# Row-wise softmax over a large vocabulary: stores on ScalarE's queue, loads on SyncE's, hand-placed semaphores and scaling on VectorE

## The chip, the cores and the metric

The kernel runs on one core of one Trainium2 chip. The metric is device time in microseconds of one execution. The core has TensorE (not used here), VectorE (DVE), ScalarE (ACT), GpSimd (POOL), SyncE (SP) and 16 DMA engines that move data between the chip's memory (HBM) and the on-chip memory (SBUF, 128 partitions). Instructions that start a DMA sit in the in-order instruction stream of one engine; here SP's, and after the change SP's and ACT's.

## What is computed

The input is 16 x 256 rows of 32768 float32 logits; the output has the same shape.

```python
scaled = logits / temperature                      # temperature is 1.0
scaled = scaled - scaled.max(axis=-1, keepdims=True)
exp_scaled = np.exp(scaled)
out = exp_scaled / exp_scaled.sum(axis=-1, keepdims=True)
```

Input and output are 536.87 MB each, so 1073.74 MB have to pass the DMA engines once.

## The kernel before

Each row is cut into two halves of 16384 columns, and each half lies on a partition of its own, so 128 partitions hold 64 rows. That is a group; there are G = 64 groups. A group is processed as C = 2 chunks of 8192 columns: one chunk is a tile of 128 x 8192 float32, 32 KiB on each partition, 4 MiB in all. A pool holds six such tiles (`_BUFS`). A chunk is loaded, worked on in place, and stored from the same tile.

For each chunk, `exps` runs a DVE reduce (line 107) that gives the negated maximum of the 8192 columns, and an ACT exponential (line 114) over the chunk, with that maximum as bias and the sum of the exponentials as a second output. When both chunks of a group are through, `factors` finds the factor of each chunk: a DVE minimum over the two negated maxima (line 129); `combine`, a shuffle and a two-operand step that exchanges this value between the two partitions of a row (lines 84 and 87); a small ACT exponential `ee` of the chunk maximum against the row maximum (line 131); a DVE multiply-and-sum of `ee` and the chunk sums (line 138); a second `combine`, of the row sums; a reciprocal (line 149) and the product `f` of `ee` and the reciprocal (line 150). Then `scales` multiplies the chunk by its factor: the first 4096 columns on DVE (line 160, one scalar per partition), the other 4096 on ACT (a Copy with a scale, line 163).

All DMAs are issued by SP, in program order (`keep_in_program_order`): loads at line 64, stores at line 75. The list `order` sets this order: six loads first, then store 0, and from there on store i followed by load i+5. A load waits until its tile is free, that is until the store from that tile has landed; a store waits until both scalings are done. Because SP works in order, load i+5 stands behind store i, and store i+1 behind load i+5. In the first group the loads, and in the last group loads, stores, reduces, exponentials and scalings, are cut into pieces of 4096 columns (`_LAST_DMA`).

Semaphores and the order of instructions on DVE and ACT are set by the framework's scheduler; `factors` has high priority. In the middle of the run, DVE does: the reduce of a group's second chunk, the first exchange, (wait for ACT) multiply-and-sum, second exchange, reciprocal, `f`, the two scalings, and then the reduce of the next group's first chunk.

Of the kernel before, what the change touches and what calls it, by code (L numbers as in the profile page):

```python
# [6 lines left out]


_SPLIT = 2
_CW = 8192  # L10
_BUFS = 6
_PIECE = 8192
_LAST_DMA = 4096
_DVE_SHARE = 0.5


@with_exitstack
def kernel(
    ctx: ExitStack,
    tc: tile.TileContext,  # L20
    logits: bass.AP,
    temperature: bass.AP,
    out: bass.AP,
):
    nc = tc.nc
    inv_t = 1.0 / float(temperature)
    P = nc.NUM_PARTITIONS
    fp32 = mybir.dt.float32
    Exp = mybir.ActivationFunctionType.Exp
    Copy = mybir.ActivationFunctionType.Copy  # L30
    X = mybir.AxisListType.X
    A = mybir.AluOpType

    xf = logits.flatten_outer_dims()
    of = out.flatten_outer_dims()
    N, V = xf.shape
    W = V // _SPLIT
    CW = min(_CW, W)
    C = W // CW
    assert W * _SPLIT == V and CW * C == W and (N * _SPLIT) % P == 0  # L40
    x = xf.rearrange("n (h v) -> (n h) v", h=_SPLIT)
    o = of.rearrange("n (h v) -> (n h) v", h=_SPLIT)
    G = N * _SPLIT // P
    n_chunks = G * C
    n_rounds = _SPLIT.bit_length() - 1

    xpool = ctx.enter_context(tc.tile_pool(name="x", bufs=_BUFS))
    spool = ctx.enter_context(tc.tile_pool(name="stats", bufs=3))
    slots = {}
    stats = {}  # L50

    def spans(total: int, step: int) -> list[tuple[int, int]]:
        return [(s, min(step, total - s)) for s in range(0, total, step)]

    def piece(g: int) -> int:
        return _PIECE if g < G - 1 else min(_PIECE, _LAST_DMA)

    def load(i: int) -> None:
        g, c = divmod(i, C)
        xs = xpool.tile([P, CW], fp32, tag="x", name="xs")  # L60
        slots[i] = xs
        for s, n in spans(CW, _LAST_DMA if g in (0, G - 1) else CW):
            tc.keep_in_program_order(
                nc.sync.dma_start(  # L64
                    out=xs[:, s : s + n],
                    in_=x[g * P : (g + 1) * P, c * CW + s : c * CW + s + n],
                )
            )

    def store(i: int) -> None:  # L70
        g, c = divmod(i, C)
        xs = slots.pop(i)
        for s, n in spans(CW, _LAST_DMA if g == G - 1 else CW):
            tc.keep_in_program_order(
                nc.sync.dma_start(  # L75
                    out=o[g * P : (g + 1) * P, c * CW + s : c * CW + s + n],
                    in_=xs[:, s : s + n],
                )
            )

    def combine(v, op) -> None:
        for j in range(n_rounds):
            mask = [i ^ (1 << j) for i in range(32)]
            nc.vector.stream_shuffle(  # L84
                out=v[:, j + 1 : j + 2], in_=v[:, j : j + 1], mask=mask
            )
            nc.vector.tensor_tensor(  # L87
                out=v[:, j + 1 : j + 2],
                in0=v[:, j : j + 1],
                in1=v[:, j + 1 : j + 2],  # L90
                op=op,
            )

    def exps(i: int) -> None:
        g, c = divmod(i, C)
        xs = slots[i]
        ps = spans(CW, piece(g))
        K = C * len(ps)
        if c == 0:
            stats[g] = tuple(  # L100
                spool.tile([P, K], fp32, tag=f"{nm}{K}", name=nm)
                for nm in ("nm", "ssum", "ee", "f", "ttj")
            )
        nm, ssum = stats[g][:2]
        for j, (s, n) in enumerate(ps):
            k = c * len(ps) + j
            nc.vector.tensor_reduce(  # L107
                out=nm[:, k : k + 1], in_=xs[:, s : s + n], axis=X, op=A.max, negate=True
            )
            if inv_t != 1.0:  # L110
                nc.vector.tensor_scalar_mul(
                    out=nm[:, k : k + 1], in0=nm[:, k : k + 1], scalar1=inv_t
                )
            nc.scalar.activation(  # L114
                out=xs[:, s : s + n],
                in_=xs[:, s : s + n],
                func=Exp,
                bias=nm[:, k : k + 1],
                scale=inv_t,
                accum_out=ssum[:, k : k + 1],  # L120
            )

    def factors(g: int) -> None:
        nm, ssum, ee, f, ttj = stats[g]
        nMh = spool.tile([P, 1 + n_rounds], fp32, tag="nMh", name="nMh")
        Sh = spool.tile([P, 1 + n_rounds], fp32, tag="Sh", name="Sh")
        rS = spool.tile([P, 1], fp32, tag="rS", name="rS")
        with tc.high_priority():
            nc.vector.tensor_reduce(out=nMh[:, 0:1], in_=nm, axis=X, op=A.min)  # L129
            combine(nMh, A.min)  # L130
            nc.scalar.activation(  # L131
                out=ee,
                in_=nm,
                func=Exp,
                bias=nMh[:, n_rounds : n_rounds + 1],
                scale=-1.0,
            )
            nc.vector.tensor_tensor_reduce(  # L138
                out=ttj,
                in0=ee,  # L140
                in1=ssum,
                scale=1.0,
                scalar=0.0,
                op0=A.mult,
                op1=A.add,
                accum_out=Sh[:, 0:1],
            )
            combine(Sh, A.add)
            nc.vector.reciprocal(out=rS, in_=Sh[:, n_rounds : n_rounds + 1])  # L149
            nc.vector.tensor_scalar_mul(out=f, in0=ee, scalar1=rS)  # L150

    def scales(i: int) -> None:
        g, c = divmod(i, C)
        xs = slots[i]
        f = stats[g][3]
        ps = spans(CW, piece(g))
        for j, (s, n) in enumerate(ps):
            k = c * len(ps) + j
            cut = int(n * _DVE_SHARE) // 512 * 512
            nc.vector.tensor_scalar_mul(  # L160
                out=xs[:, s : s + cut], in0=xs[:, s : s + cut], scalar1=f[:, k : k + 1]
            )
            nc.scalar.activation(  # L163
                out=xs[:, s + cut : s + n],
                in_=xs[:, s + cut : s + n],
                func=Copy,
                scale=f[:, k : k + 1],
            )

    order = [("L", i) for i in range(min(_BUFS, n_chunks))] + [("S", 0)]  # L170
    for i in range(1, n_chunks):
        order.append(("S", i))
        if i + _BUFS - 1 < n_chunks:
            order.append(("L", i + _BUFS - 1))

    nxt = 0
    done = -1
    loaded = 0
    for kind, i in order:
        if kind == "L":  # L180
            load(i)
            loaded = i + 1
        else:
            g = i // C
            if g > done:
                while nxt < (g + 1) * C:
                    assert nxt < loaded
                    exps(nxt)
                    nxt += 1
                factors(g)  # L190
                done = g
            scales(i)
            store(i)


# [33 lines left out]
```

## Time and profile before

| | |
|---|---|
| Time, median of 3 runs | 2495.66 us (2494.19 to 2496.56) |
| Profiled execution: span, first to last instruction | 2493.8 us (the profile gives no other time of it) |
| Instructions | 2234 |
| DVE busy | 1487.4 us, 60% of the span |
| ACT busy | 1405.0 us, 56% of the span |
| DMA, mean over the span | 431 GB/s |
| DVE reduce, 128x8192 (line 107) | 8682 ns each |
| ACT exponential, 128x8192 (line 114) | 7121 ns each |
| DVE scaling, 128x4096 (line 160) | 2350 ns each |
| ACT scaling, 128x4096 (line 163) | 3701 ns each |
| Store of 4 MiB, issue to landing | 38.2 us (median) |
| Load of 4 MiB, issue to landing | 29.0 us (median) |

How to read it: the span is the time between the first and the last instruction of one profiled execution. "Busy" is the time in which an engine ran a compute instruction; issuing a DMA or waiting is not counted. "DMA share" in a stretch is the mean share in which the 16 DMA engines had a packet under way. In this kernel a data packet is one partition's run of a tile, 32 KiB for a whole chunk. q1 is the queue on which SP issues; q14 carries instructions. The chain of work is followed back from the last instruction to what released it, step by step. Times in stretches and timelines count from the start of the span.

### The profile page before, as it was taken

What the parts mean: (1) busy time and instruction counts of PE and PEld (TensorE: products, weight loads), DVE (VectorE), ACT (ScalarE), POOL (GpSimd) and SP (SyncE); (2) the same over time, 40 slices, a digit from 0 to 9 for tenths busy, and PEclk for the clock granted to TensorE, in tenths of its full rate; (3) what the DMA queues carried; (4) which work ended last, traced back from release to release, by engine and by line L of the source; (5) the groups of instructions that cost most, each with busy time, mean ns of one, the idle gap of its engine ahead of it and who ended that gap; (6) DMA issues with size and microseconds to landing.
All of it is one profiled execution on the core that took longest, in us unless ns stands there. A gap on an engine that the chain in (4) does not pass through costs nothing.

```text
span 2493.8 us, 2234 instructions
## 1 busy us (share of the span) xinstructions
DVE 1487.4 (60%) x964; ACT 1405.0 (56%) x455; POOL 0.2 (0%) x4
## 2 busy tenths in 40 slices
DVE  7655565556655566555665566655666566655663
ACT  5665554655556555565555655555546555465553
POOL 0000000000000000000000000000000000000000
DMA  9999999999999999999999999999999999999998
GB/s 412 433 430 432 429 431 432 433 433 434 433 434 432 435 432 435 432 435 431 436 431 435 432 434 433 434 433 433 433 433 433 433 433 434 434 433 434 432 431 368
DMA packets 37745, 1073.90 MB, mean 431 GB/s; under 512 B 4192, under 2 KB 4192, under 8 KB 4192
## 3 DMA queue, kind: packets, MB, share of 16 engines
q1 hardware_dynamic: 37728, 1073.76, 99.9%
q14 instruction: 17, 0.14, 0.0%
HBM read 536.87 MB, written 536.87 MB: 431 GB/s over the span
## 4 chain that ended last, share of the span: by engine, by line
DMA 96%; SPq 1%; ACT 1%; DVE 1%; issue 1%; ACTq 0%
DMA out_dram<-xs 93%; DMA xs<-in_logits_dram 2%; SPq L64 1%; DVE nm L107 1%; ACT xs L163 1%; ACT xs L114 0%; ACTq L224 0%; SPq L75 0%; DVE f L150 0%; ACT ee L131 0%; DVE rS L149 0%; DVE Sh L87 0%; DVE ttj L138 0%; DVE Sh L84 0%; DVE Sh L138 0%
## 5 line engine op out<-in xcount | busy, mean ns | idle before, releaser
L114 ACT ACTIVATE xs<-xs,nm 128x8192 f32<-128x8192 f32 (+1 forms) x130 | 912.1, 7016 | 972.4 <-DVE nm L107 972.4
L107 DVE TENSOR_REDUCE nm<-xs 128x1 f32<-128x8192 f32 (+1 forms) x130 | 1111.6, 8551 | 527.3 <-DMA xs<-in_logits_dram 527.3
L163 ACT ACTIVATE xs<-xs,f 128x4096 f32<-128x4096 f32 (+1 forms) x130 | 468.1, 3648 | 71.4 <-DVE f L150 71.4
L160 DVE TENSOR_SCALAR xs<-xs,f 128x4096 f32<-128x4096 f32 (+1 forms) x130 | 295.7, 2318 | 3.7 <-DVE f L150 1.8
L138 DVE CUSTOM_DVE_ANT_0 ttj<-ee,ssum 128x2 f32<-128x2 f32 x64 | 10.3, 161 | 423.8 <-ACT ee L131 423.8
L114 ACT ACTIVATION_READ_ACCUMULATOR xs<-xs,nm 128x1 f32 x130 | 24.2, 186 | 0.0
L131 ACT ACTIVATE ee<-nm,nMh 128x2 f32<-128x2 f32 x64 | 17.9, 280 | 0.0
L150 DVE TENSOR_SCALAR f<-ee,rS 128x2 f32<-128x2 f32 x64 | 14.6, 229 | 2.2
L149 DVE RECIPROCAL rS<-Sh 128x1 f32<-128x1 f32 x64 | 10.5, 164 | 2.2
L87 DVE TENSOR_TENSOR nMh<-nMh 128x1 f32<-128x1 f32 x64 | 10.2, 160 | 2.2
L87 DVE TENSOR_TENSOR Sh<-Sh 128x1 f32<-128x1 f32 x64 | 10.2, 160 | 2.2
L129 DVE TENSOR_REDUCE nMh<-nm 128x1 f32<-128x2 f32 x64 | 9.9, 155 | 2.2
L84 DVE STREAM_SHUFFLE nMh<-nMh 128x1 f32<-128x1 f32 x64 | 9.7, 151 | 0.0
L84 DVE STREAM_SHUFFLE Sh<-Sh 128x1 f32<-128x1 f32 x64 | 9.7, 151 | 0.0
L114 ACT ACT_TABLE_LOAD x1 | 1.3, 1283 | 12.9 <-DMA xs<-in_logits_dram 12.9
L138 DVE DVE_READ_ACCUMULATOR2_ANT Sh<- 128x1 f32 x64 | 5.3, 84 | 0.0
L84 DVE LOAD_MASK_SELECT Sh<-Sh x64 | 0.9, 14 | 2.8
L84 DVE LOAD_MASK_SELECT nMh<-nMh x64 | 0.9, 14 | 2.7
L210 POOL MEMSET const-bfloat16-1.0<- 128x1 bf16 x1 | 0.1, 102 | 0.0
L210 POOL MEMSET const-uint8-127<- 128x1 uint8 x1 | 0.1, 102 | 0.0
L210 POOL MEMSET const-float32-0.0<- 128x1 f32 x1 | 0.1, 99 | 0.2 <-issue 0.2
L210 POOL MEMSET const-float32-1.0<- 128x1 f32 x1 | 0.1, 99 | 0.0
## 6 DMA issues: line engine op xcount, KB each, us to landing
out_dram<-xs SPq DMA_DIRECT2D x126, 4096.0 KB, 38.2
xs<-in_logits_dram SPq DMA_DIRECT2D x124, 4096.0 KB, 29.0
xs<-in_logits_dram SPq DMA_DIRECT2D x8, 2048.0 KB, 22.3
out_dram<-xs SPq DMA_DIRECT2D x4, 2048.0 KB, 26.7
```

Of the source, the lines that this page charges most:

```text
L64: nc.sync.dma_start(out=xs[:, s : s + n], in_=x[g * P : (g + 1) * P, c * CW + s : c * CW + s + n],)
L84: nc.vector.stream_shuffle(out=v[:, j + 1 : j + 2], in_=v[:, j : j + 1], mask=mask)
L87: nc.vector.tensor_tensor(out=v[:, j + 1 : j + 2], in0=v[:, j : j + 1], in1=v[:, j + 1 : j + 2], op=op,)
L107: nc.vector.tensor_reduce(out=nm[:, k : k + 1], in_=xs[:, s : s + n], axis=X, op=A.max, negate=True)
L114: nc.scalar.activation(out=xs[:, s : s + n], in_=xs[:, s : s + n], func=Exp, bias=nm[:, k : k + 1], scale=inv_t, accum_out=ssum[:, k : k + 1],
L129: nc.vector.tensor_reduce(out=nMh[:, 0:1], in_=nm, axis=X, op=A.min)
L131: nc.scalar.activation(out=ee, in_=nm, func=Exp, bias=nMh[:, n_rounds : n_rounds + 1], scale=-1.0,)
L138: nc.vector.tensor_tensor_reduce(out=ttj, in0=ee, in1=ssum, scale=1.0, scalar=0.0, op0=A.mult, op1=A.add, accum_out=Sh[:, 0:1],)
L149: nc.vector.reciprocal(out=rS, in_=Sh[:, n_rounds : n_rounds + 1])
L150: nc.vector.tensor_scalar_mul(out=f, in0=ee, scalar1=rS)
L160: nc.vector.tensor_scalar_mul(out=xs[:, s : s + cut], in0=xs[:, s : s + cut], scalar1=f[:, k : k + 1])
L163: nc.scalar.activation(out=xs[:, s + cut : s + n], in_=xs[:, s + cut : s + n], func=Copy, scale=f[:, k : k + 1],)
```

## The change

- The tile framework's scheduling is switched off for the body (`tile_critical`); the six chunk buffers, the statistics and all semaphores are allocated by hand. `Stream` stands for an engine's own semaphore, counted up by one by each of its compute instructions, and leaves out a wait that an earlier wait already covers. `Landing` stands for a DMA semaphore: two per buffer for loads (one per piece of 4096 columns), one per buffer for stores.
- Stores are issued by ACT instead of SP. ACT's order in a group is: two exponentials, `ee`, (wait for the first scaling) store, (wait for the second) store.
- Loads alone stay on SP. Load i+6 waits for the landing of store i, from the same buffer, and for nothing else.
- One exchange per group: negated maxima and sums of a group lie side by side in one tile `t`, and one shuffle gives each partition its partner's maxima and sums. The minimum, `ee` and the multiply-and-sum then run over both halves' values (4 columns, 8 in the last group), and the second exchange and the product `f` are gone.
- Scaling is done by DVE alone, over the whole 8192 columns, with two scalars per partition in one instruction: `ee` of the chunk and the reciprocal of the row sum.
- DVE's program order in a group is: reduce, reduce, shuffle (after the second exponential), minimum, (wait for `ee`) multiply-and-sum, reciprocal, scaling, scaling.

The core of the diff, the new load, store and group code, with what it replaces:

```diff
-    def load(i: int) -> None:
+    def load(i):
         g, c = divmod(i, C)
-        xs = xpool.tile([P, CW], fp32, tag="x", name="xs")
...
+        b = i % _BUFS
+        sp.wait(*freed[b])
...
+            lane = loads[b][k]
+            lane.add(
                 nc.sync.dma_start(
-                    out=xs[:, s : s + n],
-                    in_=x[g * P : (g + 1) * P, c * CW + s : c * CW + s + n],
+                    out=X[:, b * _CW + s : b * _CW + s + n],
+                    in_=x[rows, c * _CW + s : c * _CW + s + n],
...
+    def store(i):
...
-                nc.sync.dma_start(
-                    out=o[g * P : (g + 1) * P, c * CW + s : c * CW + s + n],
-                    in_=xs[:, s : s + n],
+            act.wait(scaled[i, s])
+            stores[b].add(
+                nc.scalar.dma_start(
+                    out=o[rows, c * _CW + s : c * _CW + s + n],
+                    in_=X[:, b * _CW + s : b * _CW + s + n],
...
+        freed[b] = [stores[b].token()]
...
+        dve.wait(sums[-1])
+        sh = dve.done(
+            nc.vector.stream_shuffle(out=t[:, 2 * K : 4 * K], in_=t[:, 0 : 2 * K], mask=swap)
+        )
+        dve.wait(sh)
+        mx = dve.done(
             nc.vector.tensor_reduce(
...
+                out=r[:, 0:1], in_=tv[:, :, 0, :], axis=mybir.AxisListType.XY, op=A.min
...
-            combine(Sh, A.add)
-            nc.vector.reciprocal(out=rS, in_=Sh[:, n_rounds : n_rounds + 1])
-            nc.vector.tensor_scalar_mul(out=f, in0=ee, scalar1=rS)
...
-            nc.vector.tensor_scalar_mul(
-                out=xs[:, s : s + cut], in0=xs[:, s : s + cut], scalar1=f[:, k : k + 1]
-            )
-            nc.scalar.activation(
-                out=xs[:, s + cut : s + n],
-                in_=xs[:, s + cut : s + n],
-                func=Copy,
-                scale=f[:, k : k + 1],
-            )
...
+        rc = dve.done(nc.vector.reciprocal(out=r[:, 2:3], in_=r[:, 1:2]))
+        dve.wait(rc)
...
+                scaled[i, s] = dve.done(
+                    nc.vector.tensor_scalar(
+                        out=xs,
+                        in0=xs,
+                        scalar1=e[:, k : k + 1],
+                        scalar2=r[:, 2:3],
+                        op0=A.mult,
+                        op1=A.mult,
...
-    order = [("L", i) for i in range(min(_BUFS, n_chunks))] + [("S", 0)]
-    for i in range(1, n_chunks):
-        order.append(("S", i))
-        if i + _BUFS - 1 < n_chunks:
-            order.append(("L", i + _BUFS - 1))
...
+    for i in range(_BUFS):
+        load(i)
+    for g in range(G):
+        compute(g)
+        for c in range(C):
+            i = g * C + c
             store(i)
+            j = i + _BUFS
+            if j < n_chunks:
+                load(j)
+    sp.wait(*[s.token() for s in stores])
```

## The prediction

> **What bounds the kernel now.** I read the page's queue part first, then the chain, then the middle and the end of the span, then the small chain between two scalings.
>
> From the page, the queue part and the chain's row by engine:
>
> ```profile
> q1 hardware_dynamic: 37728, 1073.76, 99.9%
> q14 instruction: 17, 0.14, 0.0%
> ...
> DMA 96%; SPq 1%; ACT 1%; DVE 1%; issue 1%; ACTq 0%
> ```
>
> One queue keeps all 16 DMA engines at work for 99.9% of the span, while DVE is busy 60% and ACT 56%. The middle in stretches (DVE, ACT, POOL busy; clock; DMA share; GB/s):
>
> ```profile
> 2.70:40.00 37.30, 25.52 (x7) 15.90 (x6) 0.00 (x0) 1.00 1.00 430
> 42.00:82.00 40.00, 36.70 (x22) 38.36 (x12) 0.00 (x0) 1.00 1.00 420
> 82.00:470.00 388.00, 227.72 (x146) 215.92 (x70) 0.00 (x0) 1.00 1.00 432
> 470.00:1000.00 530.00, 320.80 (x210) 299.74 (x97) 0.00 (x0) 1.00 1.00 433
> 1000.00:1500.00 500.00, 297.36 (x195) 284.93 (x91) 0.00 (x0) 1.00 1.00 433
> ```
>
> Loads alone (2.7 to 40) move 430 GB/s (436 if one counts from 12.9 to 42); loads and stores in turn move 433. The engines are the limit in both, and mixing directions inside one queue costs nothing. At 433 GB/s the 1073.74 MB need 2480 us, so 14 of the 2493.8 us lie at the ends. The end shows most of them:
>
> ```profile
> 2444.00:2462.00 18.00, 10.66 (x17) 15.47 (x9) 0.00 (x0) 1.00 1.00 433
> 2462.00:2482.00 20.00, 0.00 (x0) 0.00 (x0) 0.00 (x0) 1.00 0.99 423
> 2482.00:2486.00 4.00, 0.00 (x0) 0.00 (x0) 0.00 (x0) 1.00 0.47 201
> 2486.00:2490.00 4.00, 0.00 (x0) 0.00 (x0) 0.00 (x0) 1.00 0.12 53
> 2490.00:2493.80 3.80, 0.00 (x0) 0.00 (x0) 0.00 (x0) 1.00 0.04 17
> ```
>
> Nothing waits for compute here; the rate dies away because the 16 DMA engines finish at different times. The trace's landing records say the same: the 16 shares of the first load land within 0.4 us, those of the last store within 10.5 us. After 2482 only 4×201 + 4×53 + 3.8×17 = 1081 kB move, 2.5 us of work for 16 engines, spread over 11.8. **Lateness of the slowest DMA engine costs 9.3 us**; a start of 2.7 us before the first packet and about 1 us after the last make up the rest.
>
> Where the lateness comes from: the chain's steps on a store are 38.2 us, but every 310 us one is 0.8 us longer:
>
> ```profile
> 1018.31 38.28 DMA out_dram<-xs
> 1057.08 39.02 DMA out_dram<-xs
> 1096.55 38.25 DMA out_dram<-xs
> ```
>
> Packets of the instruction queue (17, of 8 KB each) lie beside these steps, at 758, 1069, 1379, 1689, 2000 and 2310 us: one per 310 us, or 8 groups of 38.7. I put them down to DVE, which has the most instructions (964/64 = 15 a group, 120 in 8 groups); that is an inference. Some eight of them make about 6 us of the lateness; the other 4 or 5 came between 120 and 470 us, in steps I cannot name.
>
> **Part by part.**
>
> *Loads past the stores on SP.* Between 200 and 2380 us SP waits for nothing but the landing of a store (2075.9 us in 112 waits); the store behind that load is issued 0.09 us after it. Undoing the order lets stores start earlier, but four transfers of 4 MB always lie in the queue (a landing takes 38.2 us, one transfer 9.7). Gain in the middle: 0.
>
> Can the new order run dry? Of six slots, those not in compute are in a queue. A slot is in compute from its landing to its store's issue. With the durations worked out below, the first chunk's store goes out 8.68 + 7.12 + 1.2 + 4.49 = 21.5 us after the second chunk has landed, the second's at 26.0; the first chunk landed one interval of 19.4 earlier. So 40.9 and 26.0 us, together 67 of every 38.7: on average 1.7 slots. Over four transfers stay queued, as now. Gain or loss 0; without the cover, each dry us is one us.
>
> *Stores on ACT.* Two issues a group at SP's 0.34 to 0.43 us, and ACT now waits in order for each scaling. Behind that wait stand the next group's exps, which need a reduce that DVE starts only after the same scalings and that takes 8.68 us. Cost 0. ACT loses 130 Copy scalings (468.1 us), which were under the DMA: gain 0.
>
> *Scaling on DVE.* Two rows of the page, by shape: 4096 columns take 2350 ns, 2048 take 1282, so 8192 take 2.35 + 2×1.07 = 4.49 us with one scalar per partition. The new form has two. No row shows it: the lower bound is 4.49, the upper the plain reduce over the same 8192 columns, 8.68. I take 4.49, because operation, type and tile are those of the nearer row. DVE's group is now a serial chain. In the tail of the before trace the second reduce ends at 2414.39, the exp at 2421.5, and the scaling begins at 2422.88, 1.37 later; the second exchange (0.39) and the factor (0.26) leave it, one shuffle and one minimum (0.19 each) and two handovers (0.03 each) enter it: 1.2. So 2×8.68 + 7.12 + 1.2 + 2×4.49 = **34.7 us a group, against 38.7 of DMA**. It is hidden with 4 us to spare.
>
> *The end.* Load 127 goes out when store 121 has landed; stores 122 to 125 then remain, less at most two while loads 126 and 127 move: at least 19.4 us of transfers. From the last landing to the first stored piece: 4.41 + 3.71 + 0.2 + 1.2 + 2.35 = 11.9 us; then a piece every 2.35, against 4.8 of transfer. No gap: 0.
>
> *Two queues instead of one.* No row shows two data queues on one engine. Bounds: 436 GB/s (12.9 to 42, loads only) gives 1073.74/436 − 1073.74/433 = −17 us; 420 GB/s (42 to 82, where the first stores meet the loads) gives +77. The nearest row is the steady 433: with shares spread by 6 to 10 us and a transfer of 9.7, some DMA engines read while others write already. I take 0.
>
> The Trainium skill ("DMA: Bandwidth & Descriptors", Issuing engines are not separate DMA queues) speaks against a gain: all issuers share the 16 DMA engines, and only issue time is saved. The trace shows issue time of 0.8 us per chunk, off the path. The same page (Latency and other measured facts) has copies through both queues at 214 GB/s each way; by that the estimate would be 1073.74/428 + 14 = 2523 us. The row's 433, from one queue, is above it.
>
> *Barriers.* A critical section adds one at each end; SP's waits for one at the existing start and end are 0.7 and 0.6 us: +1.3.
>
> *Instructions.* DVE goes from 15 to about 10 a group, so some five fetches instead of eight at 0.8 us on the late DMA engine: −2.3.
>
> **Sum:** 2493.8 + 1.3 − 2.3 = 2492.8 of span. The profile gives no other time of its execution; the median of the runs shown, 2495.66, stands 1.9 above its span, so I forecast 2494 (2494.7, rounded down as the unexplained lateness is likelier to shrink than the fast DMA engines are to wait). About 0.2%, 5 us, is what a measurement can tell from no change.
>
> **Rivals.**
>
> *The lateness shrinks, or packets gain* (faster). For it: 4 to 5 us of the lateness grew in the first 470 us, when the DMA engines ran in step and all changed direction together; two queues end that. Against: nothing shows its cause, and 433 is near the best rate shown (436). No lateness at all would give 2493.8 + 1.3 − 9.3 + 1.9 = 2488; the 436 GB/s of the loads alone would take 17 more, 2471. I put this case at 2488.
>
> *Two queues cost per packet* (slower). Place: every 32 KB packet boundary, where one DMA engine now changes queue and direction. 2048 packets each pass a DMA engine; 2.4 ns on a packet of 1213 is 5 us, the point from which it decides. For it: the 420 GB/s when stores first meet loads, with packets up to 2 us. Against: 433 when they alternate per transfer, and in that stretch both compute engines were busy 92% and more. At 420 throughout 2571; at half, 2530.
>
> *DVE becomes the bound* (slower). If the two-scalar scaling runs at the reduce's rate: 17.4 + 7.1 + 1.2 + 17.4 = 43 us a group, 64 of them 2755, plus 13 before the first reduce and some 15 after the last scaling: about 2783. It decides from (38.7 − 25.7)/2 = 6.5 us a scaling.
>
> *It doesn't decouple.* If the new queues wait for each other after all, the old order returns with the same full queue: the forecast's number.
>
> **How the numbers follow.** Forecast 0.42 (its own range 2491 to 2500, with the case that nothing decouples); lateness or packets 0.30, 2477 to 2490.6; two queues cost 0.22, 2501 to 2571, most of it under 2530; DVE binds 0.06. The range 2477 to 2530 reaches down to 2494 − 17 and leaves out DVE, the upper part of the packet case and a bit below: under 2 in 10. Faster 0.30, same 0.42, slower 0.28.
>
> **What would show it.** Right: two data queues of equal bytes, together near 99%, 433 GB/s in the middle; a scaling near 4.5 us; DVE still waiting for loads; a last slice with the same dying rate. Wrong: a middle at 425 or less (packets cost), DVE without waits for loads and DMA slices below 9 (DVE binds), a last 12 us that stay at 400 GB/s (lateness gone).

## The result and the profile after

The changed kernel takes 2497.77 us (median of 20 runs, 2497.27 to 2498.78) against 2494.72 us of the kernel before (20 runs, 2493.49 to 2496.56): a ratio of 1.0013, interval 1.0007 to 1.0019. It is slower by 3 us. That is within the 0.2% that the prediction called no change, but beyond the scatter of the runs, and on the other side of the kernel before than the forecast of 2494.

The profiled execution took 2497.72 us, its span is 2495.9. From its page: span, DVE, the rate in 40 slices, queues, and issues with their time to landing:

```profile
span 2495.9 us, 1288 instructions
...
DVE 1723.7 (69%) x644; ACT 944.5 (38%) x325; POOL 0.2 (0%) x4
...
GB/s 412 432 433 435 430 436 430 436 430 436 432 434 435 431 435 430 436 431 434 435 431 436 429 437 430 436 432 433 435 430 435 431 436 432 434 434 431 435 433 337
...
q1 hardware_dynamic: 19008, 536.88, 49.9%
q10 hardware_dynamic: 18720, 536.88, 49.8%
...
out_dram<-xs ACTq DMA_DIRECT2D x126, 4096.0 KB, 49.4
xs<-in_logits_dram SPq DMA_DIRECT2D x124, 4096.0 KB, 26.6
```

Two data queues carry half the bytes each, and the middle slices keep the rate of before. The last slice fell from 368 to 337. A middle stretch, then the end in a finer cut (DVE, ACT, POOL busy; clock; DMA share; GB/s):

```profile
470.00:1000.00 530.00, 368.07 (x140) 198.95 (x68) 0.00 (x0) 1.00 1.00 433
```

```profile
2444.00:2462.00 18.00, 4.56 (x2) 3.80 (x2) 0.00 (x0) 1.00 1.03 444
2462.00:2466.00 4.00, 4.00 (x1) 0.00 (x0) 0.00 (x0) 1.00 0.17 74
2466.00:2474.00 8.00, 3.65 (x9) 4.10 (x3) 0.00 (x0) 1.00 0.01 4
2474.00:2482.00 8.00, 6.66 (x3) 0.00 (x0) 0.00 (x0) 1.00 0.96 406
```

From 2463 us on the DMA engines run out of work, the last of them at 2468, and nothing moves until 2474: a hole that the kernel before does not have (there the engines are busy 99% from 2462 to 2482). The timeline says for whom they wait (start, duration, engine, line, what; in brackets the idle time before and what ended it):

```profile
2446.90 4.42 DVE L156 TENSOR_REDUCE t<-xs 128x1 f32<-128x4096 f32 x1 [8.87 <-DMA xs<-in_logits_dram]
...
2461.86 4.42 DVE L156 TENSOR_REDUCE t<-xs 128x1 f32<-128x4096 f32 x1 [10.54 <-DMA xs<-in_logits_dram]
2466.31 3.71 ACT L170 ACTIVATE xs<-xs,t 128x4096 f32<-128x4096 f32 x1 [11.15 <-DVE t L156]
...
2471.28 9.38 DVE L221 TENSOR_SCALAR xs<-xs,ee,row 128x4096 f32<-128x4096 f32 x4
2473.73 7.31 ACTq L128 DMA_DIRECT2D out_dram<-xs  x4
```

The last half chunk lands at 2461.8 us; before it was 2444.5. The compute behind it takes 11.9 us, as worked out in the prediction, and the last of the older stores is gone at 2467.9.

The landing records of the last transfers (us from the span's start; of the 16 DMA engines the first and the last to finish its share):

```
                      changed kernel       whole last loads (first experiment)
load 126, 1st half    2413.5  2417.8       whole: 2418.4  2423.1
load 126, 2nd half    2428.0  2432.3
load 127, 1st half    2442.6  2446.9       whole: 2437.8  2442.5
load 127, 2nd half    2457.1  2461.8
store 122             2422.5  2426.9       2429.2  2435.2
store 123             2437.1  2441.4       2443.8  2448.5
store 124             2451.6  2456.4       2453.4  2458.2
store 125             2463.1  2467.9       2463.1  2467.9
last piece stored     2494.6  2494.7       2482.6  2487.3
```

In the left columns a half load, 2 MB, lands every 14.55 us, and a whole store, 4 MB, every 14.55 us as well. A half load has 8 packets of 16 KB for each DMA engine, a store 8 packets of 32 KB; at 1.213 us for 32 KB, 8 × (0.607 + 1.213) = 14.56. So the two queues take turns **packet by packet, not byte by byte**, and the halved loads get a third of the bytes. Whole transfers taking turns would give the same 14.55 us, but the packet records show the finer turns: between 2443.0 and 2450.3 us, 15 or 16 load packets and 16 or 17 store packets start in every 1.82 us, on 16 DMA engines. Theory P, tested below, is that this alone opens the hole.

The Trainium skill ("DMA: Bandwidth & Descriptors", Queues, rings and completion order) says that a DMA engine takes its queues in turn, a packet each. The 14.55 us agree with it, if one partition's run of 16 or 32 KB is the packet.

### The profile page after: what moved, and what is told of

It is laid out like the page before. It is cut to its first block, busy times and chain, and to the rows that moved or that the text cites. A ratio compares the mean times of both kernels' runs of the same rounds, so it can differ in the third digit from the quotient of the medians.

```text
span 2495.9 us, 1288 instructions
## 1 busy us (share of the span) xinstructions
DVE 1723.7 (69%) x644; ACT 944.5 (38%) x325; POOL 0.2 (0%) x4
## 4 chain that ended last, share of the span: by engine, by line
DMA 62%; another core or an unknown queue 15%; DVE 15%; ACT 7%; SPq 0%; issue 0%; DVEq 0%
DMA out_dram<-xs 38%; DMA xs<-in_logits_dram 23%; DVE t L156 9%; ACT xs L170 7%; DVE xs L221 5%; SPq L112 0%; ACT ee L194 0%; DVE row L212 0%; DVE row L187 0%; DVE t L183 0%; DVE junk L200 0%; DVE row L200 0%; SPq L273 0%; DVEq L31 0%
## 5 line engine op out<-in xcount | busy, mean ns | idle before, releaser
L170 ACT ACTIVATE xs<-xs,t 128x8192 f32<-128x8192 f32 (+1 forms) x130 | 912.1, 7016 | 1498.5 <-DVE t L156 1498.5
L156 DVE TENSOR_REDUCE t<-xs 128x1 f32<-128x8192 f32 (+1 forms) x130 | 1111.1, 8551 | 263.8 <-DMA xs<-in_logits_dram 263.8
L221 DVE TENSOR_SCALAR xs<-xs,ee,row 128x8192 f32<-128x8192 f32 (+1 forms) x130 | 576.6, 4478 | 2.3
L194 ACT ACTIVATE ee<-t,row 128x4 f32<-128x4 f32 x64 | 19.0, 297 | 27.0 <-DVE row L187 27.0
L200 DVE CUSTOM_DVE_ANT_1 junk<-ee,t 128x4 f32<-128x4 f32 x64 | 10.4, 163 | 23.3 <-ACT ee L194 23.3
L170 ACT ACTIVATION_READ_ACCUMULATOR xs<-xs,t 128x1 f32 x130 | 24.2, 186 | 0.0
L212 DVE RECIPROCAL row<-row 128x1 f32<-128x1 f32 x64 | 10.5, 164 | 2.2
L187 DVE TENSOR_REDUCE row<-t 128x1 f32<-128x4 f32 x64 | 10.1, 157 | 2.2
L183 DVE STREAM_SHUFFLE t<-t 128x4 f32<-128x4 f32 x64 | 9.9, 155 | 0.0
L200 DVE DVE_READ_ACCUMULATOR2_ANT row<- 128x1 f32 x64 | 5.3, 82 | 0.0
```

The source lines that it names most:

```text
L156: nc.vector.tensor_reduce(out=t[:, k : k + 1], in_=xs, axis=mybir.AxisListType.X, op=A.max, negate=True)
L170: nc.scalar.activation(out=xs, in_=xs, func=Exp, bias=t[:, k : k + 1], scale=inv_t, accum_out=t[:, K + k : K + k + 1],)
L183: nc.vector.stream_shuffle(out=t[:, 2 * K : 4 * K], in_=t[:, 0 : 2 * K], mask=swap)
L187: nc.vector.tensor_reduce(out=r[:, 0:1], in_=tv[:, :, 0, :], axis=mybir.AxisListType.XY, op=A.min)
L194: nc.scalar.activation(out=ev, in_=tv[:, :, 0, :], func=Exp, bias=r[:, 0:1], scale=-1.0)
L200: nc.vector.tensor_tensor_reduce(out=j_[:, 0 : 2 * K].rearrange("p (a k) -> p a k", a=2), in0=ev, in1=tv[:, :, 1, :], scale=1.0, scalar=0. ...
```

## The experiments

Medians and ratios are against the kernel before, measured beside each version on the same chip (its medians there lie between 2494.6 and 2494.8 us).

**Whole last loads.** In the changed kernel the last group's loads are no longer cut:

```diff
-        pieces = spans(_CW, _EDGE if g in (0, G - 1) else _CW)
+        pieces = spans(_CW, _EDGE if g == 0 else _CW)
```

> The last group's two loads go out whole (8192 columns, packets of 32 KB) instead of in halves (16 KB packets); reduces, exponentials and stores of that group stay in halves. Theory P (a DMA engine serves its two queues one packet at a time, so half-size load packets beside whole store packets get a third of the bytes; the last loads come late, the stores run out, and the DMA engines stand idle from about 2464 to 2474 us): the two loads then share evenly, the last lands near 2442 instead of 2461.8, the first store piece goes out near 2458 (two reduces of 4.4 us now follow the landing) while stores still last until 2465. No idle stretch, span near 2488, ratio to before about 0.998. Rival C (the last group is late because DVE scales alone and in a fixed order; the packet size doesn't matter): the first store piece goes out no earlier than 2474, plus up to 4.4 us for the second reduce: span 2496 to 2500, ratio 1.001 to 1.003.

Measured: 2489.81 us, ratio 0.9981, interval 0.9972 to 0.9990; span of the profile 2488.5. The right columns above are this run: the last load lands at 2442.5 although it is issued 3 us later (2415.8 instead of 2412.7), and the two loads land 19.4 us apart. The end of its span:

```profile
2462.00:2482.00 20.00, 3.63 (x2) 0.00 (x0) 0.00 (x0) 1.00 0.98 420
2482.00:2486.00 4.00, 0.00 (x0) 0.00 (x0) 0.00 (x0) 1.00 0.15 66
2486.00:2490.00 4.00, 0.00 (x0) 0.00 (x0) 0.00 (x0) 1.00 0.01 4
```

The hole is gone, though one reduce more now stands behind the last landing. Theory P holds, rival C falls. This version beats both kernels.

**Half stores.** The loads stay halved; the stores that meet them are halved too:

```diff
-        for s, n in spans(_CW, _EDGE if g == G - 1 else _CW):
-            act.wait(scaled[i, s])
+        for s, n in spans(_CW, _EDGE if g >= G - 3 else _CW):
+            act.wait(scaled.get((i, s), scaled[i, 0]))
```

> The last loads stay in halves; the stores of the two groups before the last (chunks 122 to 125) also go out in halves, so that both queues hold 16 KB packets while the last loads are under way. Compute is unchanged. Theory P: even shares, last load near 2442, first store piece 11.9 us later near 2454, stores last until about 2465: no idle stretch, span near 2488, ratio to before about 0.998. Rival C: the end is as in the changed kernel, 2496, ratio 1.001. Rival D (any smaller store packet costs time of its own): 4 more DMAs, at most 1 us.

Measured: 2490.23 us, ratio 0.9983 (0.9974 to 0.9992), span 2488.7. The load halves land 9.7 us apart instead of 14.55, the last at 2445.6, and the hole is gone:

```profile
2462.00:2482.00 20.00, 2.39 (x2) 0.00 (x0) 0.00 (x0) 1.00 1.01 432
```

Equal packets, equal shares; the median is 0.4 us above that with whole last loads, so the extra DMAs cost little. This is the cleanest of the tests, since no compute instruction differs.

**The last two stores behind the last loads.** Only the queue of stores 124 and 125 changes:

```diff
-            act.wait(scaled[i, s])
+            late = g == G - 2
+            (sp if late else act).wait(scaled[i, s])
             stores[b].add(
-                nc.scalar.dma_start(
+                (nc.sync if late else nc.scalar).dma_start(
```

> The changed kernel; only the stores of chunks 124 and 125 are issued by SP, which puts them behind the last loads in the same queue. The last loads stay in halves and still meet the whole stores 122 and 123 on ACT's queue. Theory P: up to the end of store 123, near 2441, the loads get a third; the last one and a half pieces then have the DMA engines for themselves and land near 2447; stores 124 and 125 cover 19.4 us after that, the compute after the last landing needs 11.9: no idle stretch, span near 2488.5, ratio to before about 0.998, as with whole loads or half stores. Rival C (it is the packet form as such that costs, not the order at the end): 2496, ratio 1.001.

Measured: 2490.41 us, ratio 0.9983 (0.9974 to 0.9992), span 2488.4. The last load lands at 2448.4, and stores 124 and 125 fill the time behind it:

```profile
2462.00:2482.00 20.00, 5.22 (x3) 0.00 (x0) 0.00 (x0) 1.00 0.98 422
```

The halved loads stayed, so it is not their form that costs; it is how little store work remains when the last one has landed.

**Everything but the split.** The changed kernel with the stores back in SP's queue, each ahead of a load as in the kernel before:

```diff
-            act.wait(scaled[i, s])
+            sp.wait(scaled[i, s])
             stores[b].add(
-                nc.scalar.dma_start(
+                nc.sync.dma_start(
...
-            j = i + _BUFS
-            if j < n_chunks:
+            j = i + _BUFS - 1
+            if i and j < n_chunks:
```

> The changed kernel with the stores back on SP, in the order of before (store i, then load i+5): hand-placed semaphores, one exchange and DVE-only scaling remain, one data queue. Theory P: no sharing of packets, no idle stretch at the end; the rate dies away only by lateness. If the 4 to 5 us of unnamed lateness came with the single queue, lateness is 5 x 0.9 + 4.5 = 9 us and the span 2492 to 2493; if it came with the split of the scaling or the instructions, lateness is about 4.7 and the span 2488, ratio 0.997 to 0.998. Rival C: idle stretch and 2496 as in the changed kernel.

Measured: 2493.03 us, ratio 0.9993 (0.9984 to 1.0001), span of the profile 2492.0. The end of its span:

```profile
2462.00:2482.00 20.00, 0.00 (x0) 0.00 (x0) 0.00 (x0) 1.00 0.99 424
2482.00:2486.00 4.00, 0.00 (x0) 0.00 (x0) 0.00 (x0) 1.00 0.61 262
2486.00:2490.00 4.00, 0.00 (x0) 0.00 (x0) 0.00 (x0) 1.00 0.15 66
```

No hole, but the rate dies away late again: 7.2 us between the first and the last DMA engine (9 expected for a single queue), 4.9 of it already there at 382 us. In the changed kernel it is 1.0 us at that time. So the lateness that the prediction could not name goes with the single queue in these traces. The scatter of the runs fits: the spans of this kernel lie between 2488.8 and 2492.2, those of the kernel before between 2490.5 and 2494.4, those of the version with two queues and whole last loads between 2487.9 and 2488.5. Why engines on one queue drift apart between 150 and 480 us stays open.

**The split alone.** The kernel before, framework and all, with one word changed:

```diff
-                nc.sync.dma_start(
+                nc.scalar.dma_start(
                     out=o[g * P : (g + 1) * P, c * CW + s : c * CW + s + n],
```

> The kernel before, with stores issued by ACT instead of SP and nothing else by hand (the scheduler places them; exchange, scaling on both engines and semaphores as before). Theory P: the split alone makes the loss: the last loads in halves get a third of the bytes, the last load lands near 2460, idle DMA for about 9 us near the end, span about 2495, ratio about 1.001. The lateness of the slowest DMA engine, 10.5 us before and 4.7 after, shows here as the instruction fetches of before (8 x 0.8 = 6 us) if the queue split took the unnamed 4 us away, and as 10 us if it did not. Rival C (DVE-only scaling makes the loss): ratio 1.000, no idle stretch at the end.

Measured: 2925.75 us, ratio 1.1728 (1.1712 to 1.1744). No theory expected that, and it does not isolate the split: with the store on ACT the scheduler also placed other instructions anew. From the timeline:

```profile
412.81 8.69 DVE L107 TENSOR_REDUCE nm<-xs 128x1 f32<-128x8192 f32 x1 [22.70 <-DMA xs<-in_logits_dram]
421.41 0.15 DVE L138 CUSTOM_DVE_ANT_0 ttj<-ee,ssum 128x2 f32<-128x2 f32 x1
...
422.46 4.62 DVE L160 TENSOR_SCALAR xs<-xs,f 128x4096 f32<-128x4096 f32 x2
...
436.28 0.29 ACT L131 ACTIVATE ee<-nm,nMh 128x2 f32<-128x2 f32 x1 [6.51 <-DVE nMh L87]
436.34 0.34 ACTq L75 DMA_DIRECT2D out_dram<-xs  x1
```

Counting reduces, loads and stores from the start of the run, DVE's multiply-and-sum at 421.41 belongs to group 8 and now stands behind the reduce of the first chunk of group 10. That reduce waits 22.7 us for its load, and the load had waited for a slot, that is for a store of group 7, which had been held up in the same way. ACT's second store of group 8 stands behind the `ee` of group 10, 6.6 us after its scalings are done (422.46 + 7.31). DMA share falls to 0.87, the rate to 365 GB/s between 400 and 860 us. The expectation failed on the assumption that a scheduler leaves the rest as it was. The split is judged by the changed kernel and its versions against the previous experiment, where the compute is the same.

**More instructions on DVE.** In every group but the last, small memsets of a scratch tile follow the scalings:

```diff
+        if g < G - 1:
+            for q in range(10):
+                nc.vector.memset(pad[:, q : q + 1], 0.0)
```

Ten a group, on the version with whole last loads:

> The variant with whole last loads (span 2488.5), and 10 small DVE memsets of a scratch tile more in every group but the last: DVE goes from 10 to 20 instructions a group, some 1 to 2 us a group, which the 4 us of slack cover. Theory F (each instruction fetch of DVE holds up one DMA engine, always the same, by 0.9 us): 10 fetches instead of 5, lateness 9.4 instead of 4.7 us, span 2493, 4.6 us more than without the padding. Rival G (lateness has another cause, and the fetches only fall beside it): span 2488.5, lateness 4.7.

Measured: 2497.21 us, ratio 1.0011 (1.0002 to 1.0020), spans 2492.8 to 2499.1. Ten a group, on the changed kernel:

> The changed kernel itself with the same 10 memsets a group. Theory P and F together: lateness doubles to 9.4 us, but the end is set by the compute behind the last load and not by the queue. The slowest DMA engine is 4.7 us later with the last load, so the end moves by about 4.7, to 2500 to 2501; the faster ones stand idle longer. If instead only the slowest engine's stores set the end and the idle stretch absorbs its lateness, span 2496 to 2497. Rival G: 2496, lateness 4.7.

Measured: 2504.37 us, ratio 1.0040 (1.0027 to 1.0052), spans 2502.1 to 2504.1. Five a group (5 in place of 10 in the diff), on the version with whole last loads:

> As the padded variant with whole last loads, but 5 memsets a group instead of 10: 15 DVE instructions a group, as many as the kernel before has, so about 8 fetches. With 10 memsets the lateness came out at 15.3 us on the loads and 5 on the stores of the slowest DMA engine, not at 9.4, and the idle stretch came back. Theory F, one price for each fetch (0.93 us): lateness 7.4 us on both, span 2491. Theory F2 (some fetches also put the engine's loads one packet of 1.2 us further behind its stores): loads later than stores by 1 to 4 packets, span between 2491 and 2494, scattered from run to run. Rival G (not the fetches): 2488.5.

Measured: 2492.07 us, ratio 0.9990 (0.9981 to 0.9999), spans 2490.1 to 2490.6.

With five, the end is near theory F: eight DVE fetches (packets at 310 to 350 us from each other), 6.6 us between the first and the last DMA engine at the end (7.4 expected), 2.3 us more span than without the padding. But on the way the slowest engine's stores landed 8.3 us late and its loads 4.5, where F had the same for both. With ten, the direction is right and the size isn't: in the profiled run, the slowest of its 11, the last stores and the last load landed 15.1 to 15.5 us late where 9.4 was expected. Up to 2390 us only the stores were so late, and the loads about 5 (the expectation for the run with five has loads and stores the other way round). The last load landed at 2459 instead of 2442, and the hole opened again:

```profile
2462.00:2482.00 20.00, 15.65 (x12) 7.90 (x5) 0.00 (x0) 1.00 0.45 191
```

Ten fetches at 0.93 make 9.3; the rest, and what sets an engine's stores so far behind its loads, is not shown. Nor is it one DMA engine alone: at the end the second was 10.8 us late and the third 6.7. On the changed kernel the padding moved the span by 6.7 us from median to median (2495.9 to 2502.6): there the late engine delays the last load (2470.0 instead of 2461.8 in the profiled run), and so the hole's end; 4.7 were expected.

## Why the prediction was wrong

The new scaling's row (number of instructions, then busy us and mean ns of one):

```profile
L221 DVE TENSOR_SCALAR xs<-xs,ee,row 128x8192 f32<-128x8192 f32 x126 | 567.2, 4544 | 2.3
```

The sum, step by step, against the profile (spans 2493.8 to 2495.9):

- **The end: this is the step that failed.** The prediction let stores 122 to 125 remain "less at most two while loads 126 and 127 move: at least 19.4 us of transfers". It counted shares by bytes. By packets, four half loads pass while four whole stores pass: on the first DMA engine 6.0 us of store 125 remained when its share of the last load had landed (2457.1 to 2463.1), in place of at least 19.4. With whole loads 25.4 us remained (2437.8 to 2463.1). The need after the last landing was right, 11.9 us. The first DMA engine stood idle from 2463.1 to 2473.7, 10.6 us, and the restart cost 1.3 more (the first piece landed 6.1 us after its issue, a piece takes 4.86): +11.9, forecast 0. Whole loads, half stores and two stores moved each took the hole away.
- **Lateness and instructions: mis-sized.** Forecast −2.3. The five DVE fetches came true (four of them some 504 us apart, and at each of these the latest engine falls 0.9 us further behind), and the unnamed rest vanished with the second queue: 4.7 us before the last pieces in place of 10.5. At the very end only 0.2 us are left, because every engine waits in the hole: −10.3. The rival "lateness shrinks" had the right effect, that two queues end the early drift, and a near price, 2488 us for no lateness at all; the hole hid it. Without the hole 2489.8 us were measured. That the drift came from all engines changing direction together is not shown.
- **Two queues at no cost per packet: right.** 433 GB/s in the middle, and the first DMA engine takes 77.45 us for eight landings before and after.
- **Barriers: mis-sized**, 0.2 us at the start (first load at 0.94 instead of 0.73) and 0.25 at the end, forecast 1.3.
- **Scaling on DVE: right.** 4544 ns each, forecast 4.49 us, so the second scalar costs next to nothing; group after group the scalings start 34.6 us apart where DVE sets the pace (40.17, 74.77, 109.36), forecast 34.7, and later DVE waits about 4 us a group for loads. The rival in which DVE becomes the bound falls.
- **No dry stretch in the middle, stores on ACT at no cost: right** by the 39 slices.

Together 2492.8 + 11.9 − 8.0 − 0.8 = 2495.9, the span measured. That the forecast missed by only 3.8 us is luck: two errors, of +11.9 and about −9, nearly cancelled. The prediction put its doubt on the rate of two queues, for which it had no row, and none on who gets which share of it, for which it had none either.

As parts of the time, by medians: everything but the split −1.6 us (2493.0, not clear of zero), the second queue with whole last loads −3.2 more (2489.8; −2.8 with halved loads and half stores), halved last loads beside whole stores +8.0 (2497.8).

## What to carry to other kernels

When loads and stores share DMA engines through two queues, work out who gets which share at the end of the run: packets of equal size shared equally here, and cutting the last loads finer cost 8 us beside a second queue with whole packets (what it gains or costs in one queue was not measured). What counts at the end is how much store work is left when the last load has landed, against the compute that follows it. A split of queues is best tried where the order of instructions is written by hand; a scheduler may answer it by moving other instructions.

## What the runs showed that was not expected

DVE instructions cost DMA time in this kernel: in the runs without added instructions the latest DMA engine falls 0.8 to 1.0 us further behind at nearly every 8 KB packet of DVE's instructions. (The records do not name the engines; that it is the same one each time is read from the spread alone.) Five more tiny instructions a group cost 2.3 us, ten cost 5 to 11, while DVE has slack in both. And in both traces with a single queue the 16 DMA engines drift apart by some 5 us early in the run; with two queues they don't, unless ten instructions a group are added: then the spans scatter over 6.3 us, more than with one queue.
